# A two-layer diffusion backbone on one core: norm sums by tokens on partitions, two final products on GpSimd, and another place for the weight order FOURS

## The chip, the cores and the metric

The kernel runs on one core of one Trainium2 chip. The metric is device time in microseconds, the median of several executions. A profiled execution gives, besides, a trace of each engine: PE (TensorE; PEld is its weight load), DVE (VectorE), ACT (ScalarE), POOL (GpSimd) and SP, whose queue issues the DMAs.

## The reference

256 latent tokens and 256 context tokens of width 2048 pass an even layer (retention and a Fourier mixing, one output projection) and an odd layer (gated short convolution); the latent stream then has a final norm. All is float32. What matters here:

```python
def _rmsnorm(x, w):
    y = x * rsqrt(mean(x * x, axis=-1) + EPS)          # over the 2048 channels of one token
    return y * w
# per layer:  h = _rmsnorm(x, w) * (1 + scale) + shift
# even layer: x = x + gate * (concat(retention, fourier) @ w_out)       4096 -> 2048
# odd layer:  bg, cg, xt, g = split(h @ w_in)                           2048 -> 4 * 4096
#             x = x + gate * ((bg * conv3(cg * xt) * silu(g)) @ w_out)  4096 -> 2048
# output: _rmsnorm(x, final_norm_w)
```

## The kernel before

Activations lie transposed: channels on the 128 partitions, 256 tokens along the free axis. So a projection takes the weights as the stationary operand and the activation as the moving one. To keep float32's accuracy, each number is cut in a high part and a residue: of a weight, `whi` (ScalarE, L94) and `wlo` (VectorE, L59), each 128x512, in rings of six; of an activation, both parts side by side in a tile of 512 columns, high part first.

`group_t` computes 256 output channels. A weight load (`raw`, 1 MB, by SP, three buffers) has four pieces; a piece is one pair `whi`, `wlo`, and eight matmuls: four H (high part of the weight by all 512 columns) and four L (residue by the 256 columns of the high part). Results stand in PSUM in two halves, which `lr` adds. The order of the eight is a table: LOW is L0 H0 L1 H1 L2 H2 L3 H3, HIGH is H0 L0 H1 L1 ..., FOURS is H0 H1 H2 H3 L0 L1 L2 L3. `SETTLE` and `AFTER` name for a call which order its first piece has and which the others have; without them a call has LOW throughout.

`project` is the output projection of either layer (`w0o`, `w1o`): eight blocks of 256 channels, the first seven by `group_t` (four weight loads, 16 pieces, each), the last by `group_d`, which adds in one PSUM bank. It adds gate times result to the stream `x1` (L831) and gathers the squares for the next norm in `acc`. At the end the sum over channels is a product with a matrix of ones, which leaves the sum of each token in all partitions (128x256, bank `tot`); `rstd_bc` takes the root (ScalarE, L206) and the reciprocal (VectorE, L207). In the first layer the row then enters `modulate` (L213 to L215), which makes the input `h` of the second layer's projection `w1` (16 blocks of four groups `tcg`, `txt`, `tbg`, `tg`, eight pieces each). In the second layer it multiplies the stream into `fo` (L62, L920), and eight DMAs (L922), issued by SP in program order, write the output. `fo` is in ring `t2` of five buffers.

During the first layer and its output projection, background tasks read the matrices `adaT` (VectorE, L388) for the gates. The order of instructions on each engine is set by a scheduler from the program, with its own estimate of times; each engine then runs its list in order.

Of the kernel before, what the change touches and what calls it, by code (L numbers as in the profile page):

```python
# [20 lines left out]
D = 2048  # L21
# [3 lines left out]
P = 128  # L25
# [10 lines left out]
def body(tc, a, out):  # L36
    nc = tc.nc
    es = ExitStack()
    with es:
# [9 lines left out]
        def bank(name):  # L49
            return ap.tile([P, 512], F32, tag="bk", name=name)  # L50
# [77 lines left out]
        HIGH = "H0 L0 H1 L1 H2 L2 H3 L3".split()  # L128
        FOURS = "H0 H1 H2 H3 L0 L1 L2 L3".split()

        SETTLE, AFTER = (HIGH, FOURS), (HIGH, LOW)

        def group_t(wd, i0, nkt, streams, orders=(LOW, LOW)):

            ps = [psum("gT") for _ in streams]
            last = nkt * 8 - 1
            for kt in range(nkt):
                raw = load_raw(wd[i0 + kt])
                bg()
                for pc, (hi, lo) in enumerate(split_w(raw)):  # L140
                    todo = orders[kt + pc > 0]
                    seen = set()
                    for what, j in ((x[0], int(x[1])) for x in todo):
                        k2, m = j // 2, j % 2
                        kc, c0 = kt * 8 + pc * 2 + k2, j * 128
                        n = 512 if what == "H" else 256
                        w = (hi if what == "H" else lo)[:, c0:c0 + 128]
                        for t, st in zip(ps, streams):
                            mm(t[:, m, 0:n], w, st[kc // 2][:, kc % 2, 0:n], kc == 0 and j not in seen,
                               kc == last and j in seen)  # L150
                        seen.add(j)
                    if pc % 2:
                        hook()
            return ps
# [667 lines left out]

        finish_mods(0, 16)
        l1 = es.enter_context(tc.tile_pool(name="l1", bufs=1))
        x1 = [l1.tile([P, 2, 256], F32, name=f"x1_{b}") for b in range(8)]

        def project(wd, xs, gcol, xin, acc, first=None, post=None):


            def res(b, m, v, src):  # L830
                nc.vector.scalar_tensor_tensor(x1[b][:, m, :], v, mods[:, gcol + 2 * b + m:gcol + 2 * b + m + 1],  # L831
                                               src[:, m, :], op0=ALU.mult, op1=ALU.add)

            tot = None
            for b in range(8):
                src = xin(b)
                quiet[0] = b >= 7 - (post is not None)
                if b < 7:
                    t = first if b == 0 and first is not None else group_t(wd, 4 * b, 4, [xs], *({1: (SETTLE,), 2: (AFTER,)}.get(b, ())))[0]
                    s = lr(l1, t)  # L840
                    for m in range(2):
                        res(b, m, s[:, m, :], src)
                    if b == 0:
                        nc.scalar.square(acc[:], x1[b][:])
                    else:
                        sq = l1.tile([P, 2, 256], F32, tag="t2", bufs=5, name="sq")
                        nc.scalar.square(sq[:], x1[b][:])
                        add(acc[:], acc[:], sq[:])
                    for m in range(2 if post is not None else 0):
                        nc.scalar.activation(x1[b][:, m, :], x1[b][:, m, :], AF.Copy,  # L850
                                             scale=cols[:, post + 2 * b + m:post + 2 * b + m + 1])
                else:
                    t = group_d(wd, 4 * b, 4, xs)
                    tot = bank("tot")
                    for m in range(2):
                        mm(tot[:, 0:256], ones[:], acc[:, m, :], m == 0, False)

                    warm = l1.tile([P, 1], F32, tag="warm", name="warm")
                    nc.scalar.activation(warm[:], acc[:, 0, 0:1], AF.Sqrt)
                    sq = l1.tile([P, 2, 256], F32, tag="t2", bufs=5, name="sq")  # L860
                    for m in range(2):
                        res(b, m, t[:, m * 256:m * 256 + 256], src)
                        nc.scalar.square(sq[:, m, :], x1[b][:, m, :])
                        mm(tot[:, 0:256], ones[:], sq[:, m, :], False, m == 1)
            return rstd_bc(l1, tot[:, 0:256], D)

        def reload(b):
            xr = l1.tile([P, 2, 256], F32, tag="t2", bufs=5, name="xr")
# [14 lines left out]
        w1 = a["w1"]  # L883
        y1 = []
        for b in range(16):
            tcg, = group_t(w1, b * 8, 2, [h1], *((SETTLE,) if b in (1, 2) else ()))
            scg = lr(l1, tcg, "scg", 2)
            txt, = group_t(w1, b * 8 + 2, 2, [h1], *((AFTER,) if b in (1, 2) else ()))
            z = lr(l1, txt, "z", 2)
            mul(z[:], z[:], scg[:])  # L890
            cv = l1.tile([P, 2, 256], F32, tag="cv", bufs=2, name="cv")
            for m in range(2):
                w = [cols[:, C_CV + j * 32 + 2 * b + m:C_CV + j * 32 + 2 * b + m + 1] for j in range(3)]
                z4 = z[:, m, :].rearrange("p (r w) -> p r w", w=64)
                c4 = cv[:, m, :].rearrange("p (r w) -> p r w", w=64)
                nc.vector.tensor_scalar(cv[:, m, :], z[:, m, :], w[1], None, op0=ALU.mult)
                nc.vector.scalar_tensor_tensor(c4[:, :, 1:64], z4[:, :, 0:63], w[0], c4[:, :, 1:64],
                                               op0=ALU.mult, op1=ALU.add)
                nc.vector.scalar_tensor_tensor(c4[:, :, 0:63], z4[:, :, 1:64], w[2], c4[:, :, 0:63],
                                               op0=ALU.mult, op1=ALU.add)  # L900
            tbg, = group_t(w1, b * 8 + 4, 2, [h1])
            sbg = lr(l1, tbg)
            mul(cv[:], cv[:], sbg[:])
            tg, = group_t(w1, b * 8 + 6, 2, [h1])
            sg = silu_lr(l1, tg, "t2", 5)
            mul(cv[:], cv[:], sg[:])
            y1.append(act_tile(YA[b] if b < 8 else f"hx{b - 8}", f"y1_{b}"))
            split_act(y1[b], cv[:])
            quiet[0] = False

        finish_mods(48, 64)
        acc1 = l1.tile([P, 2, 256], F32, tag="acc", name="acc1")
        rs2 = project(a["w1o"], y1, 48, lambda b: x1[b], acc1, post=C_FNW)
        for b in range(8):
            o = l1.tile([P, 2, 256], F32, tag="t2", bufs=5, name="fo")
            if b < 7:
                mul(o[:], x1[b][:], rs2[:].unsqueeze(1).to_broadcast([P, 2, 256]))
            else:
                for m in range(2):
# [20 lines left out]
def _layout(i):  # L940
# [37 lines left out]
    wu = w0[:, uo:uo + 2048].reshape(2048, 8, 256)  # L978
    m = np.concatenate([[128], np.arange(255, 128, -1)])
    wu = np.stack([wu[:, :, 0:128], wu[:, :, m]], axis=1)  # L980
    a["w0m"] = wu[:, :, :, 0].reshape(16, P, 2, 8).transpose(1, 0, 2, 3)
    wu = wu.reshape(8, 2, P, 2, 2, 4, P).transpose(4, 0, 2, 1, 3, 5, 6)
    a["w0u"] = wu.reshape(16, P, 2048)
# [49 lines left out]
```

## Time and profile before

| | |
|---|---|
| median of 3 runs | 1823.37 us (1822.88, 1823.37, 1826.58) |
| profiled execution | 1826.86 us; its span, first to last instruction, 1825.1 us |
| busy share of PE, DVE, ACT, POOL | 97%, 68%, 49%, 0% |
| granted TensorE clock | 0.988 |
| first layer's output projection, blocks 1 to 7 | about 763 to 914 us of the span |
| first layer's closing norm and `modulate` | 914 to 937 us |
| `w1` / `w1o` | 920 to about 1630 / to 1812 us |
| closing norm and output | 1812 to 1825 us |

A row of a group reads: line, engine, operation, what it writes <- reads, shapes, count, then busy us, mean ns of one, and idle time of the engine before it with what ended it. A row of a stretch gives its bounds, its length, busy us with the number of instructions, the granted clock, the busy share of the DMA engines and their GB/s.

### The profile page before, as it was taken

Reading aid. Unit: us, or ns where it says so; the run is one execution under the profiler, and the core shown is the slowest. Engines: PE = TensorE matmul, PEld = TensorE weight load, DVE = VectorE, ACT = ScalarE, POOL = GpSimd, SP = SyncE. Lnnn points to the kernel's source line nnn. Section 1 sums busy time; section 2 is a strip of 40 time slices with the busy share of each in tenths; the row PEclk is TensorE's granted clock in tenths of the full one; section 3 lists DMA queues with packets and bytes.
Section 4 is the critical chain, followed back from the end, with each engine's and each line's share of the span. In section 5 each row is a group of like instructions: output and inputs, shape, how many; then the busy total and the mean of one; then the engine's idle time right before and its main releaser. Section 6 shows DMA issues by size and latency. Waiting matters only on the chain.

```text
span 1825.1 us, 25950 instructions
## 1 busy us (share of the span) xinstructions
PE 1777.8 (97%) x10086; PEld 1514.6 (83%) x10086; DVE 1248.0 (68%) x2001; ACT 901.9 (49%) x1493; POOL 0.2 (0%) x4
## 2 busy tenths in 40 slices
PE   5999999999989999999999999999999999999997
PEld 3667888888877888888978888888888888888887
DVE  5348858758469788777677888666666666665554
ACT  4225626345455455444555555555555555555553
POOL 0000000000000000000000000000000000000000
PEclk9999999999989899999999999999999999999999
DMA  9886656655435556577647777555555555555552
GB/s 388 341 315 259 233 212 221 240 207 208 166 117 217 199 188 216 194 295 295 231 155 264 296 277 281 197 191 185 187 196 195 185 185 191 197 189 185 187 193 105
DMA packets 58732, 400.82 MB, mean 220 GB/s; under 512 B 6512, under 2 KB 6896, under 8 KB 11376
## 3 DMA queue, kind: packets, MB, share of 16 engines
q1 hardware_dynamic: 58608, 399.16, 59.8%
q8 instruction: 79, 1.29, 0.3%
q14 instruction: 45, 0.37, 0.1%
HBM read 397.03 MB, written 2.10 MB: 219 GB/s over the span
## 4 chain that ended last, share of the span: by engine, by line
PE 94%; DVE 3%; DMA 1%; ACT 1%; issue 0%; SPq 0%; DVEq 0%; ACTq 0%
PE gT L56 71%; PE gN L56 7%; PE gD L56 3%; PE pu L56 2%; PE gemv L56 2%; PE o L56 2%; PE pk L56 1%; PE pvx L56 1%; PE pvc L56 1%; PE pd L56 1%; DMA raw<-ada 1%; PE S L56 1%; PE pq L56 1%; DVE wlo L59 1%; PE pP L56 1%; PE py L56 0%
## 5 line engine op out<-in xcount | busy, mean ns | idle before, releaser
L94 ACT CAST whi<-raw 128x512 fp32r<-128x512 f32 x1024 | 628.3, 620 | 627.3 <-PE gT L56 469.4
L59 DVE TENSOR_TENSOR wlo<-raw,whi 128x512 fp32r<-128x512 f32 x1024 | 693.2, 688 | 344.4 <-ACT whi L94 334.5
L56 PE MATMUL gT<-h,whi 128*128 128x512 f32 x2048 | 707.6, 394 | 0.7 <-DVE h L215 0.7
L56 PE MATMUL gT<-h,wlo 128*128 128x256 f32 x2048 | 560.8, 278 | 3.4 <-ACT h L214 3.4
L56 PEld LDWEIGHTS gT<-h,whi 128*128 128x128 f32 x2048 | 383.3, 188 | 89.0 <-DVE h L215 1.2
L56 PEld LDWEIGHTS gT<-h,wlo 128*128 128x128 f32 x2048 | 383.4, 188 | 5.6 <-ACT h L214 3.8
L56 PE MATMUL gT<-hx,whi 128*128 128x512 f32 x576 | 209.4, 398 | 0.0
L388 DVE CUSTOM_DVE_ANT_0 raw<-raw,scb 128x2048 f32<-128x2048 f32 x64 | 146.5, 2290 | 54.0 <-DMA raw<-adaT 50.8
L56 PE MATMUL gT<-hx,wlo 128*128 128x256 f32 x576 | 165.2, 287 | 2.8 <-ACT v L507 1.6
L56 PE MATMUL gT<-y,whi 128*128 128x512 f32 x448 | 150.9, 394 | 0.0
L56 PEld LDWEIGHTS gT<-hx,whi 128*128 128x128 f32 x576 | 108.8, 189 | 21.3
L56 PEld LDWEIGHTS gT<-hx,wlo 128*128 128x128 f32 x576 | 109.5, 190 | 10.0 <-DVE wlo L59 2.7
L56 PE MATMUL gT<-y,wlo 128*128 128x256 f32 x448 | 116.9, 278 | 0.0
L56 PEld LDWEIGHTS gT<-y,whi 128*128 128x128 f32 x448 | 82.9, 188 | 18.2
L198 ACT COPY lr_r<-gT 128x512 f32<-128x512 f32 x103 | 60.5, 587 | 65.7 <-PE gT L56 65.4
L56 PEld LDWEIGHTS gT<-y,wlo 128*128 128x128 f32 x448 | 82.1, 188 | 1.4
L56 PE MATMUL gT<-yA,whi 128*128 128x512 f32 x224 | 77.5, 398 | 0.0
L56 PE MATMUL gT<-yB,whi 128*128 128x512 f32 x224 | 76.9, 398 | 0.0
L65 DVE TENSOR_TENSOR t<-gT,lr_r 128x512 f32<-128x512 f32 x68 | 46.9, 689 | 29.9 <-ACT lr_r L198 29.7
L56 PE MATMUL gT<-yA,wlo 128*128 128x256 f32 x224 | 59.9, 281 | 0.6 <-DVE wlo L59 0.6
L56 PE MATMUL gN<-whi,hx 128*128 128x512 f32 x192 | 59.7, 392 | 0.0
L56 PE MATMUL gN<-whi,hc 128*128 128x512 f32 x192 | 59.7, 391 | 0.0
(283 smaller groups left out, 2162.0 us busy)
## 6 DMA issues: line engine op xcount, KB each, us to landing
raw<-w SPq DMA_DIRECT2D x168, 1024.0 KB, 4.8
raw<-adaT SPq DMA_DIRECT2D x64, 1024.0 KB, 4.9
raw<-ada SPq DMA_DIRECT2D x32, 1024.0 KB, 7.1
raw<-w0o SPq DMA_DIRECT2D x32, 1024.0 KB, 4.8
raw<-w1o SPq DMA_DIRECT2D x32, 1024.0 KB, 4.8
raw<-w0g SPq DMA_DIRECT2D x16, 1024.0 KB, 4.8
raw<-w0u SPq DMA_DIRECT2D x16, 1024.0 KB, 4.9
raw<-w0s SPq DMA_DIRECT2D x8, 1024.0 KB, 5.6
```

Source lines behind the costliest of these rows:

```text
L56: nc.tensor.matmul(o, l, r, start=start, stop=stop, skip_group_check=True)
L59: nc.vector.tensor_tensor(o, x, hi.bitcast(F32), op=ALU.subtract)
L65: nc.vector.tensor_tensor(o, x, y, op=ALU.add)
L94: nc.scalar.copy(hi, x)
L198: nc.scalar.copy(r[:], t[:, :, 256:512])
L388: nc.vector.tensor_tensor_reduce(out=raw[:], in0=raw[:], in1=scb[:], scale=1.0, scalar=0.0, op0=ALU.mult, op1=ALU.add, accum_out=gv[:, j:j ...
```

## The change

Three things. First, the closing norm of both layers: the squares are now the stationary operand and one column of ones the moving one, so a token's sum stands on a partition (128x2, one column for each half of the tokens). Root and reciprocal are taken of that, and the row is brought back to all partitions by two products with an identity matrix `eye` (a new input, loaded once), which leave it in PSUM (`tot[:, 256:512]`), where `modulate` and the final products read it. Second, at the end ScalarE copies the row to SBUF (`rsb`), and GpSimd computes the final products of blocks 1 and 4. Third, `SETTLE` and `AFTER` become lists of eight orders, one for each piece, and stand elsewhere: in `project` in blocks 3 and 4 (eight pieces SETTLE, eight AFTER) instead of 1 and 2, in `w1` in groups `tbg`, `tg` of blocks 0 and 1 besides `tcg`, `txt` of blocks 1 and 2.

```diff
-        SETTLE, AFTER = (HIGH, FOURS), (HIGH, LOW)
+        SETTLE, AFTER = [HIGH] + [FOURS] * 7, [HIGH] + [LOW] * 7
...
-                    todo = orders[kt + pc > 0]
+                    todo = orders[(kt * 4 + pc) % len(orders)]
...
+        eye = l1.tile([P, P], F32, name="eye")
+        nc.sync.dma_start(eye[:], a["eye"])
...
-                    t = first if b == 0 and first is not None else group_t(wd, 4 * b, 4, [xs], *({1: (SETTLE,), 2: (AFTER,)}.get(b, ())))[0]
+                    t = first if b == 0 and first is not None else group_t(wd, 4 * b, 4, [xs], SETTLE + AFTER if b in (3, 4) else (LOW,))[0]
...
+                    def sums(x, fst, lst):
+                        for h in range(2):
+                            mm(tot[:, h:h + 1], x[:, h * 128:h * 128 + 128], ones[:, 0:1], fst and h == 0, lst)
+
                     for m in range(2):
-                        mm(tot[:, 0:256], ones[:], acc[:, m, :], m == 0, False)
+                        sums(acc[:, m, :], m == 0, False)
...
-                        mm(tot[:, 0:256], ones[:], sq[:, m, :], False, m == 1)
-            return rstd_bc(l1, tot[:, 0:256], D)
+                        sums(sq[:, m, :], False, m == 1)
+            r = l1.tile([P, 2], F32, tag="rcol", bufs=2, name="rcol")
+            nc.scalar.activation(r[:], tot[:, 0:2], AF.Sqrt, bias=eps[:], scale=1.0 / D)
+            nc.vector.reciprocal(r[:], r[:])
+
+            for h in range(2):
+                mm(tot[:, 256 + h * 128:384 + h * 128], r[:, h:h + 1].to_broadcast([P, P]), eye[:], True, True)
+            return tot[:, 256:512]
...
-            tcg, = group_t(w1, b * 8, 2, [h1], *((SETTLE,) if b in (1, 2) else ()))
+            tcg, = group_t(w1, b * 8, 2, [h1], SETTLE if b in (1, 2) else (LOW,))
...
-            txt, = group_t(w1, b * 8 + 2, 2, [h1], *((AFTER,) if b in (1, 2) else ()))
+            txt, = group_t(w1, b * 8 + 2, 2, [h1], AFTER if b in (1, 2) else (LOW,))
...
-            tbg, = group_t(w1, b * 8 + 4, 2, [h1])
+            tbg, = group_t(w1, b * 8 + 4, 2, [h1], SETTLE if b in (0, 1) else (LOW,))
...
-            tg, = group_t(w1, b * 8 + 6, 2, [h1])
+            tg, = group_t(w1, b * 8 + 6, 2, [h1], AFTER if b in (0, 1) else (LOW,))
...
+        rsb = l1.tile([P, 256], F32, tag="rstd", name="rsb")
+        nc.scalar.copy(rsb[:], rs2[:])
         for b in range(8):
             o = l1.tile([P, 2, 256], F32, tag="t2", bufs=5, name="fo")
-            if b < 7:
+            if b in (1, 4):
+
+                nc.gpsimd.tensor_tensor(o[:], x1[b][:], rsb[:].unsqueeze(1).to_broadcast([P, 2, 256]), op=ALU.mult)
+            elif b < 7:
                 mul(o[:], x1[b][:], rs2[:].unsqueeze(1).to_broadcast([P, 2, 256]))
```

How it moves instructions, at three places. A row names what is written, then what is read; of a matmul the moving operand stands first, then the stationary one, then the shape of the result.

PE in the first layer's output projection, at the start of its block 3 (`gT_7096` before, `gT_7098` after; `yA` is the layer's activation). Before, first two pieces in part:

```order
L56 MATMUL gT_7096<-yA0_1510,wlo_7103 128x256
L56 MATMUL gT_7096<-yA0_1510,whi_7102 128x512
L56 MATMUL gT_7096<-yA0_1510,wlo_7103 128x256
L56 MATMUL gT_7096<-yA0_1510,whi_7102 128x512
L56 MATMUL gT_7096<-yA0_1510,wlo_7103 128x256
L56 MATMUL gT_7096<-yA0_1510,whi_7102 128x512
```

After, the end of the first piece and the next two:

```order
L56 MATMUL gT_7098<-yA0_1510,whi_7104 128x512
L56 MATMUL gT_7098<-yA0_1510,wlo_7105 128x256
L56 MATMUL gT_7098<-yA1_1514,whi_7108 128x512 x4
L56 MATMUL gT_7098<-yA1_1514,wlo_7109 128x256 x4
L56 MATMUL gT_7098<-yA2_2404,whi_7112 128x512 x4
L56 MATMUL gT_7098<-yA2_2404,wlo_7113 128x256 x4
```

The first piece is now HIGH and the next seven FOURS, then one HIGH and seven LOW; block 4 has the same again, and block 1, which had FOURS, has LOW.

PE after the first layer's norm, where it waits for VectorE, with the first two groups of `w1` interleaved (`gT_8322` and `gT_8427` before, `gT_8330` and `gT_8435` after; `h1_4` is a part of the modulated input, two slices of 128 channels). Before:

```order
L56 MATMUL gT_8322<-h1_4_8254,wlo_8376 128x256
L56 MATMUL gT_8322<-h1_4_8254,whi_8375 128x512
L56 MATMUL gT_8322<-h1_5_8255,wlo_8380 128x256
L56 MATMUL gT_8427<-h1_0_8250,wlo_8431 128x256
L56 MATMUL gT_8427<-h1_0_8250,whi_8430 128x512
```

After:

```order
L56 MATMUL gT_8330<-h1_4_8262,wlo_8384 128x256
L56 MATMUL gT_8435<-h1_0_8258,wlo_8439 128x256
L56 MATMUL gT_8435<-h1_0_8258,whi_8438 128x512
L56 MATMUL gT_8435<-h1_0_8258,wlo_8439 128x256
L56 MATMUL gT_8435<-h1_0_8258,whi_8438 128x512
```

The second group's first piece now stands ahead of the H matmuls of the second half of `h1_4`.

VectorE and GpSimd at the end, in the closing norm and output. VectorE before:

```order
L207 RECIPROCAL rstd_17091<-rstd_17091 128x256
L62 TENSOR_TENSOR fo_17094<-x1_0_6640,rstd_17091 128x512
L62 TENSOR_TENSOR fo_17097<-x1_1_6641,rstd_17091 128x512
L62 TENSOR_TENSOR fo_17100<-x1_2_6642,rstd_17091 128x512
L62 TENSOR_TENSOR fo_17103<-x1_3_6643,rstd_17091 128x512
L62 TENSOR_TENSOR fo_17106<-x1_4_6644,rstd_17091 128x512
```

After, VectorE's rows and, last three, all that GpSimd has after its start-up:

```order
L874 RECIPROCAL rcol_17103<-rcol_17103 128x2
L62 TENSOR_TENSOR fo_17110<-x1_0_6642,tot_17087 128x512
L62 TENSOR_TENSOR fo_17116<-x1_2_6644,tot_17087 128x512
L62 TENSOR_TENSOR fo_17119<-x1_3_6645,tot_17087 128x512
L62 TENSOR_TENSOR fo_17125<-x1_5_6647,tot_17087 128x512
L933 ISA
L933 TENSOR_TENSOR fo_17113<-x1_1_6643,rsb_17108 128x512
L933 TENSOR_TENSOR fo_17122<-x1_4_6646,rsb_17108 128x512
```

Products 1 and 4 moved to GpSimd behind a library step (`ISA`); SP's list still issues the eight outputs in the order of blocks. VectorE's product 0 waits for the semaphore count of ScalarE's copy `rsb`, as GpSimd's product 1 does; product 5 waits for the landing of output 0, product 6 for that of output 1, and the last for that of output 2.

More of the change, by code (lines that the diff above doesn't have):

```diff
@@ L129, in body, with group_t @@
         FOURS = "H0 H1 H2 H3 L0 L1 L2 L3".split()
-        SETTLE, AFTER = (HIGH, FOURS), (HIGH, LOW)
-        def group_t(wd, i0, nkt, streams, orders=(LOW, LOW)):
+        SETTLE, AFTER = [HIGH] + [FOURS] * 7, [HIGH] + [LOW] * 7
+        def group_t(wd, i0, nkt, streams, orders=(LOW,)):
             ps = [psum("gT") for _ in streams]
@@ L980, in _layout @@
     wu = np.stack([wu[:, :, 0:128], wu[:, :, m]], axis=1)
+    a["eye"] = np.eye(P, dtype=np.float32)
     a["w0m"] = wu[:, :, :, 0].reshape(16, P, 2, 8).transpose(1, 0, 2, 3)
```

## The prediction

> **What bounds the kernel now.** I read the page's busy shares and the shares of the chain that ended last first, then the chain piece by piece at the places that the change touches, then the count of matmuls in equal stretches.
>
> ```profile
> PE 1777.8 (97%) x10086; PEld 1514.6 (83%) x10086; DVE 1248.0 (68%) x2001; ACT 901.9 (49%) x1493; POOL 0.2 (0%) x4
> PE 94%; DVE 3%; DMA 1%; ACT 1%; issue 0%; SPq 0%; DVEq 0%; ACTq 0%
> ```
>
> TensorE is the bound nearly everywhere, so an edit counts in two ways only: where the chain leaves PE (the two closing norms), and where it alters the pace at which PE issues. The last norm, in the chain in order of time (start, length, what):
>
> ```profile
> 1812.20 0.49 DVE x L831
> ...
> 1812.72 0.42 ACT sq L863
> ...
> 1813.19 1.15 PE tot L56 x4
> ...
> 1814.36 0.48 ACT rstd L206
> ...
> 1814.86 1.76 DVE rstd L207
> ...
> 1816.65 2.82 DVE fo L62 x5
> ...
> 1820.90 0.48 DVE fo L920
> ```
>
> The reader sees one series without overlap; the reciprocal of 128x256 is its dearest single step. The first layer has the same series at 914.8, and after it VectorE holds PE back until 928.8, from where PE has the chain again. The last three rows are PE's: its wait in the middle of the series (in square brackets), its pace after that (busy, matmuls, clock), and its last wait for VectorE:
>
> ```profile
> 916.44 0.48 ACT rstd L206
> ...
> 916.94 1.76 DVE rstd L207
> ...
> 918.73 1.28 DVE modt L213 x3
> ...
> 928.34 0.41 DVE h L215
> ...
> 928.79 16.29 PE gT L56 x91
> 919.81 0.44 PE L56 MATMUL gT<-h,wlo 128*128 128x256 f32 x1 [3.41 <-ACT h L214]
> 920.00:923.40 3.40, 3.19 (x10) 0.50 0.00 0
> 928.79 0.50 PE L56 MATMUL gT<-h,whi 128*128 128x512 f32 x1 [0.47 <-DVE h L215]
> ```
>
> Pace of PE, from stretches counted on PE alone (us, busy, matmuls, clock, DMA):
>
> ```profile
> 785.00:885.00 100.00, 100.00 (x567) 1.00 0.79 294
> 1025.00:1125.00 100.00, 100.00 (x579) 1.00 0.76 283
> 1500.00:1600.00 100.00, 100.00 (x579) 1.00 0.54 190
> 1657.00:1677.00 20.00, 20.00 (x116) 1.00 0.53 190
> ```
>
> All four are fully busy at full clock, yet the first issues fewer matmuls. About two matmuls in each count only overlap an edge, so one takes 100/565 = 177.0 ns in the first layer's output projection and 100/577 = 173.3 ns in the second layer's input projection (second and third row); in order FOURS (last row) 20/114 = 175.4 ns. In LOW order there are thus two paces, 3.7 ns a matmul or 29 ns a piece (8 matmuls) apart. The slow one is not a shortage: DMA load is alike in the first two rows. It follows what stood before: the quick rows come after one HIGH piece, seven FOURS, one HIGH, LOW.
>
> **The change, part by part, against the profiled execution (1826.86 us, span 1825.1).**
>
> Sums by tokens. The four 128x256 products per norm become eight one-column products, each of two passes. The nearest row is the modulation's, also fp32 with 128x128 weights:
>
> ```profile
> L56 PE MATMUL gemv<-cols,gs 128*128 128x2 f32 x64 | 7.7, 242 | 0.8 <-DVE gs L287 0.8
> L56 PE MATMUL tot<-sq,ones x8: 379/379/483, 915.3 to 1813.9; 128*128 128x256 f32 x8
> L56 PEld LDWEIGHTS tot<-sq,ones x8: 186/188/190, 915.3 to 1813.7; 128*128 128x128 f32 x8
> L859 ACT ACTIVATE warm<-acc 128x1 f32<-128x1 f32 x2 | 0.4, 202 | 0.0
> L65 DVE TENSOR_TENSOR md<-gemv,cols 128x4 f32<-128x4 f32 x16 | 1.8, 157 | 8.0 <-PE gemv L56 7.8
> L207 DVE RECIPROCAL rstd<-rstd 128x256 f32<-128x256 f32 x1 | 1.8, 1753 | 1.8 <-ACT rstd L206 1.8
> L863 ACT ACTIVATE sq<-x 128x256 f32<-128x256 f32 x2 | 0.8, 416 | 8.7 <-DVE x L831 8.7
> ```
>
> Its 64 passes are eight in each of eight calls: 7.7/8 = 0.96 us a call, 0.12 a pass. The eight on the closing squares begin as before at 1813.19 and, with some 0.2 for a first load that nothing hides, end at 1814.35: no gain over 1814.34. Those on acc stand before the squares and are hidden by the residual and the square (1812.2 to 1813.1). Root over 128x2: 0.20 like the warm-up row, for 0.48. Reciprocal over 128x2: 0.17, near VectorE's row of 4 columns (157 ns), for 1.76. Its low end is 0.06; its high end, 1.75 again, holds if the price is per call, but VectorE's rows grow with their columns (157 ns for 4, 684 for 512 below). The new step: two products with the identity, four passes of 128 columns, the first load 0.19, three more starts at 0.12, and 0.31 from start to end of the last (between 242 and 379): 0.86. With three hand-overs of 0.03, the row stands in PSUM at 1814.35 + 0.20 + 0.17 + 0.86 + 0.09 = 1815.67, against 1816.62 (1814.86 + 1.76) before: -0.95 us. Bounds: four passes at the 0.38 of a 256-column one without overlap (1.5) leave -0.3; 0.5 for all four gives -1.3; a reciprocal at 1.75 would turn -0.95 into +0.6.
>
> First layer: the same -0.95, then the modulation reads the row from PSUM. VectorE's chain from 918.73 to 928.79 moves as a whole. The order puts one more weight residue ahead of the second half of h_4, but on PE one piece of the second group now fills that place, and its operand stands behind 9.8 us of VectorE work (20 steps of the modulation at 0.40, 3 residues at 0.60, the starts of this chain), where the old one stood behind 10.0. PE was there 0.47 us early before, so -0.95 stays. The identity's DMA (64 KB, issued ahead of xr on SP, which passes one w0o load) costs nothing while the weight slots are full; if a weight comes late for it, some 0.2.
>
> Second layer: the first product on VectorE does not start when the row stands. It waits for ScalarE's copy of the row, by the same semaphore value as GpSimd's product. A copy of 128x256 is near the 0.42 of the square, plus 0.06 for two hand-overs: VectorE starts at 1816.15, not 1816.65: -0.5. Were the copy free, -0.95; at the 0.59 of a 512-column copy, -0.3.
>
> GpSimd. What do two products fewer on VectorE bring (they start 0.60 apart)? The output queue answers:
>
> ```profile
> DMA  0000000000029999999999999999999700000000
> L922 SPq DMA_DIRECT2D out<-fo x8: 332/333/348, 1817.4 to 1821.8; - x8
> DMA to landing us min/median/max: 2.0/2.4/2.6
> ```
>
> The first row (40 slices of 1815 to 1826) is full from 1818.3 to 1823.5: 2.1 MB leave at the DMA engines' pace, 0.68 us per 256 KB, nearly VectorE's 0.60. Also fo has five buffers, so products 5, 6, 7 wait until outputs 0, 1, 2 have landed. Let S be the start of the products (1816.65 now) and g the time of one on GpSimd. The last output now lands at 1821.8 + 2.4 = S+7.55. SP takes the outputs in order, so output 1 and all behind it wait for GpSimd: issued at S+g, landed 2.05 later, six more at 0.69, S+g+6.2. Output 4, its second: S+2g + 2.05 + 3 x 0.69 = S+2g+4.1. The largest counts. Up to g = 1.35 GpSimd costs nothing and gains nothing. No row prices it: 0.69 (VectorE's own row, 682/684/694) is the low end, 3.5 (the reciprocal's pace for 512 columns) the high, giving 0 to +3.6. It is a plain product, nearest the low end; I take 1.3 and so 0. The Trainium skill (GPSIMD Engine Reference, Performance versus the Vector engine) puts such an operation at 1.96 times VectorE's. By it g would be an estimated 1.35 us, which changes the sum by nothing; no run here shows it yet.
>
> Fours. In w0o pieces of blocks 3 to 6 (64) were all slow. Now 14 are FOURS (175.4: 14 x 8 x 1.6 ns = -0.18), 4 HIGH (0 taken), and 46 LOW, quick if the sequence does there what it does in w1: 46 x 29 ns = -1.35 (else 0). Block 1 loses its FOURS, which other products cut apart: 0, ends 0.2 either way; block 2 stays LOW. Together -1.5. In w1, blocks 0 and 1 change 32 pieces between FOURS, slow and quick, -0.1; in w1o two FOURS stretches replace one, 0.
>
> In block 1 of w0o, PE stands for a residue that is late behind a VectorE step waiting for its DMA:
>
> ```profile
> DVE raw L388 <- DMA raw<-adaT: 2.3, 1, 2.3
> PEld gT L56 <- DVE wlo L59: 0.9, 1, 0.9
> ```
>
> LOW begins with the residue, FOURS did not, and the order of this step changes; -0.8 to +0.9, taken 0.
>
> Sum: -0.95 - 0.5 - 1.5 - 0.1 = -3.05, so 1823.8 for such an execution. The profiled one stands 3.5 above the median of 1823.37; one timed run, 1826.58, stands with it. If these are two levels of pace, the median already has some quick pieces and can't gain the 1.5 twice. The 80 pieces of w0o's blocks 2 to 6 alone hold 80 x 29 ns = 2.3 of the 3.5, so I let half of the 1.5 count: 1823.37 - 1.55 - 0.75 = 1821.1.
>
> **The rivals.**
> 1. All of it counts. The levels come from elsewhere, the order change gives its whole 1.5, and the stall of 0.8 goes: 1823.37 - 3.05 - 0.8 = 1819.5. For it: the first row's 100 us, in blocks 2 to 6, are slow throughout. Against: the unexplained level, and that the stall is a DMA's.
> 2. GpSimd is slow. At g = 3.5 the end moves by S+11.1 for S+7.55, +3.6: 1824.7. It decides from 1.35 on. For it: no row of POOL but 0.2 us of start-up. A heavier form is a start of h before GpSimd's first product: it holds output 1, SP's queue and product 6, so 1821.1 + h, slower by over 0.2% from h = 5.9; the order shows the library step at the head of POOL's program, 1800 us ahead, which speaks against it. The Trainium skill (GPSIMD Engine Reference, Instruction dispatch) speaks of about 6 us at the first call of a freshly loaded kernel, by which the sum would be an estimated 1827; no row here shows such a start.
> 3. The quick pace is lost (slower than before). Re-entering HIGH after 7 LOW pieces, where before there were 23, may leave w1 in the slow pace: blocks 2 to 15 (448 pieces) and w1o up to its own HIGH (48), 496 x 29 ns = +14.4: 1835.5. Over the 2.3 gained and 3.65 (0.2%) it decides from 205 slow pieces on. Against: by the rows at 1025 and 1500 the pace, once quick, held.
> 4. The change doesn't do what it says: four passes without overlap, a slow copy, w0o as now: -0.3 in the first norm, +0.3 in the second, so 1823.4.
>
> A rule on the clock, the row first: PE idles 3.41 us in the first norm, and the stretch behind it shows 10 matmuls in 3.4 us at clock 0.50. The Trainium skill (TensorE: Matmul & The Clock Gate, What's actually happening) says an idle window of about 3.4 us halves the clock; with the idle time cut to some 2.5 us, the drop could go by it. By the last wait PE still stood 0.47 us for VectorE afterwards, so with or without the drop the sum is the same.
>
> **How the numbers follow.** A change under 0.2% (3.65 us) can't be told from none in this kernel. Forecast 0.47, own range 1819.8 to 1822.4 (all or none of the 1.5, half of the row's bounds). Rival 1 0.30, rival 2 0.08 for slow and 0.03 for the heavy start, rival 3 0.07, rival 4 0.05. Faster by over 0.2% means under 1819.7: rival 1, 0.30. Slower, over 1827.0: rival 3 and two thirds of the heavy start, 0.09. The rest, 0.61, is within. The range reaches from 1818.3 (rival 1, the row at both its -1.3 ends, the level of the lowest run, 0.5 under the median) to 1825.4 (rival 2's slow form without w0o's part); outside it stay the heavy start, rival 3 and a few in a hundred at the low end.
>
> **What would show it.** Right: 2.2 us from the end of the first layer's last square to its first modulation step, now 3.1; VectorE's first output product behind ScalarE's copy, 0.5 after the row; DMA full through the output as now; 577 matmuls net in 100 us of w0o's late blocks and of w1. Wrong: a product of POOL over 1.35, an idle stretch in the output's transfers, slow counts in w1, a new wait of PE in block 1 of w0o.

## Result and profile after

The changed kernel takes 1835.07 us (median of 1834.48, 1835.03, 1835.11, 1838.86) against 1823.12 us for the kernel before on the same chip (1822.84, 1822.88, 1823.37, 1826.58). The ratio is 1.0066, 95% interval 1.0047 to 1.0084. The forecast was 1821.1, in a range of 1818.3 to 1825.4; the kernel became slower instead of faster, and the time lies near that of rival 3 (1835.5).

The page of the profiled execution after (1835.11 us, span 1833.3, clock 0.991), busy shares and the shares of the chain that ended last:

```profile
PE 1788.6 (98%) x10110; PEld 1520.1 (83%) x10110; DVE 1243.7 (68%) x1999; ACT 901.8 (49%) x1494; POOL 2.7 (0%) x6
PE 95%; DVE 3%; DMA 1%; ACT 1%; issue 0%; SPq 0%; DVEq 0%; ACTq 0%
```

PE is busy 10.8 us longer than before, for 24 matmuls more. Its counts in the stretches that the prediction read (us, busy, matmuls, clock, DMA):

```profile
785.00:885.00 100.00, 100.00 (x569) 1.00 0.77 286
1025.00:1125.00 100.00, 100.00 (x568) 1.00 0.75 280
1500.00:1600.00 100.00, 100.00 (x568) 1.00 0.52 184
```

All three stand near the 567 of the slow pace; before, the last two had 579. So `w0o` did not become quick, and `w1` lost the quick pace that it had. (From 1025 to 1745 us, which takes in part of `w1o`, PE has 4079 matmuls against 4154 before.)

The closing norm in the chain in order of time (start, length, what), then the output's DMA row (40 slices of 1823 to 1834) and GpSimd's group:

```profile
1822.21 1.07 PE tot L56 x8
...
1823.30 0.27 ACT rcol L873
...
1823.59 0.18 DVE rcol L874
...
1823.81 0.72 PE tot L56 x4
...
1824.56 0.38 ACT rsb L928
...
1824.96 0.70 DVE fo L62
...
1825.68 2.05 DMA out<-fo
```

```profile
DMA  0000000000001999999999999999999980000000
L933 POOL TENSOR_TENSOR fo<-x,rsb x2: 1264/1265/1266, 1825.0 to 1826.2; 128x512 f32<-128x512 f32 x2
```

The series is shorter, the stream of the output as full as before, and GpSimd's two products run beside VectorE's. The first norm, from the same view, and the clock behind it:

```profile
910.22 1.07 PE tot L56 x8
...
911.83 0.72 PE tot L56 x4
...
912.57 1.26 DVE modt L213 x3
...
914.29 15.81 PE gT L56 x74
```

```profile
913.20:920.00 6.80, 6.29 (x18) 0.50 0.00 0
```

The whole difference, by when the same instruction stands in the two traces (us):

| up to | before | after | added in the piece |
|---|---|---|---|
| first matmul of `w0o` on `yA` | 712.16 | 708.08 | -4.08 |
| end of the first norm's squares | 915.61 | 910.56 | -0.97 |
| 38th matmul of `w1` on `h` | 928.79 | 923.28 | -0.45 |
| end of the last squares | 1813.53 | 1822.55 | +14.52 |
| first product of `fo` | 1816.65 | 1824.96 | -0.71 |
| end of the span | 1825.08 | 1833.33 | -0.06 |

The first row is, as far as the traces tell, not the change: in the ten traces of kernels with the new norm this instruction stands anywhere from 707.68 to 714.55, in the four with the old one from 710.27 to 712.95. Stretches of before and then of after show another clock there:

```profile
541.20:551.30 10.10, 8.91 (x22) 0.50 0.34 112
633.40:636.70 3.30, 3.30 (x11) 0.50 0.00 0
```

```profile
541.20:551.30 10.10, 7.68 (x36) 1.00 0.44 144
633.40:636.70 3.30, 3.30 (x23) 1.00 0.14 27
```

At half clock PE did 22 matmuls for 36, and 11 for 23. Up to 715 us the trace of before has 34.1 us at half clock, that of after 17.1. Such stretches come in other lengths in each execution; they fit that the profiled execution of before stands 3.7 us over its median and that of after at it, and that of after's four runs the one with the lowest clock, 0.987, is the longest (1838.86; the others have 0.990 to 0.992). So 8.25 in the spans and 11.95 in the medians are one result, and its cause is the 14.5 us of `w1` and `w1o`. Of the second row, 0.86 goes with a wait of PE in the profiled execution of before, in `w0o`'s block 1: `norm_pool` and `before_six` (below), which have before's order in `w0o` but not the wait, take 202.59 us for this piece, before 203.45 and after 202.48.

### The profile page after: what moved, and what is told of

The parts are those of the page before. It is cut to its first block, busy times and chain, and to the rows that moved or that the text cites. A ratio compares the mean times of both kernels' runs of the same rounds, so it can differ in the third digit from the quotient of the medians.

```text
span 1833.3 us, 26023 instructions
## 1 busy us (share of the span) xinstructions
PE 1788.6 (98%) x10110; PEld 1520.1 (83%) x10110; DVE 1243.7 (68%) x1999; ACT 901.8 (49%) x1494; POOL 2.7 (0%) x6
## 4 chain that ended last, share of the span: by engine, by line
PE 95%; DVE 3%; DMA 1%; ACT 1%; issue 0%; SPq 0%; DVEq 0%; ACTq 0%
PE gT L56 71%; PE gN L56 7%; PE gD L56 3%; PE pu L56 2%; PE gemv L56 2%; PE o L56 2%; PE pvx L56 1%; PE pk L56 1%; PE pvc L56 1%; PE pd L56 1%; PE S L56 1%; PE pq L56 1%; PE pP L56 1%; PE py L56 1%; PE pz L56 1%; DVE wlo L59 1%
## 5 line engine op out<-in xcount | busy, mean ns | idle before, releaser
L59 DVE TENSOR_TENSOR wlo<-raw,whi 128x512 fp32r<-128x512 f32 x1024 | 694.3, 688 | 359.0 <-ACT whi L94 353.3
L56 PE MATMUL gT<-h,whi 128*128 128x512 f32 x2048 | 716.3, 399 | 0.1
L56 PE MATMUL gT<-yB,wlo 128*128 128x256 f32 x224 | 62.4, 281 | 0.0
```

The source lines that it names most:

```text
L56: nc.tensor.matmul(o, l, r, start=start, stop=stop, skip_group_check=True)
L59: nc.vector.tensor_tensor(o, x, hi.bitcast(F32), op=ALU.subtract)
```

## Experiments

A settle below is a run of pieces HIGH, FOURS (several), HIGH, then LOW. A pair is one L matmul and the H matmul behind it; a LOW piece has four. The kernel before was measured again beside each group of runs, so its median differs from group to group.

The expectations weigh three theories against each other. By the phase theory, the pace behind a settle depends on the pieces at which its FOURS start and end, and so on their number. By the norm theory, the new norm shifts the start of `w1` and this alone takes the quick pace. By the count theory, more settles are better, but not when they stand close together.

**Which part costs it?** Three kernels divide the change, and a fourth tries the phase theory in its first form, by which the number of FOURS decides.

`norm_pool`: the change with all tables of before (new norm row, copy, GpSimd alone).

> The changed kernel with all tables of the kernel before: the new norm sums and GpSimd's two products alone. Phase theory: w1 quick as in the kernel before; the norm gains what the profile after showed, 0.45 us at layer 1's end and 0.7 at the end of the kernel: 1821.5 to 1823. Norm theory: w1 slow, 1835 to 1838.

`orders_only`: the kernel before with the new tables alone.

> The kernel before with the new tables alone (w0o's and w1's), without the new norm sums and without GpSimd. Phase theory: no H is pulled forward in the order, all settles are HIGH and seven FOURS from a slow pace, so w1 and w1o stay slow: 13 to 15 us over the kernel before, 1836 to 1838. Norm theory: the quick pace of the kernel before is kept, 1822 to 1824.

`w1_as_before`: the change with `w1`'s two new settles taken out.

```diff
-            tbg, = group_t(w1, b * 8 + 4, 2, [h1], SETTLE if b in (0, 1) else (LOW,))
+            tbg, = group_t(w1, b * 8 + 4, 2, [h1])
-            tg, = group_t(w1, b * 8 + 6, 2, [h1], AFTER if b in (0, 1) else (LOW,))
+            tg, = group_t(w1, b * 8 + 6, 2, [h1])
```

> The changed kernel with the two w1 tables tbg and tg back to LOW, so that only tcg and txt of blocks 1 and 2 settle, as in the kernel before; the norm row, GpSimd's two products and w0o's tables stay changed. The order puts one H matmul of the HIGH piece (gT_8765 H) one piece forward again, as before. Phase theory (what the FOURS leave behind depends on the piece at which they start and end): the LOW pieces of w1 from block 1 on and of w1o go at the quick pace, 346.7 ns a pair instead of 353.3; 496 pieces by some 26 to 29 ns less than after, 13 to 14.5 us: 1820 to 1822. Norm theory (the norm's other end shifted the start of w1, and this took the quick pace): the tables do nothing, the slow pace stays, 1834 to 1836. Count theory (more settles are better, only those that stand too close to each other fail): block 1 alone at 7 LOW pieces from block 2's, some of w1 quick, 1822 to 1830.

`six_last`: one FOURS fewer in `w1`'s last settle, with a LOW piece in its place.

```diff
+        SIX = [HIGH] + [FOURS] * 6 + [LOW]
-            tcg, = group_t(w1, b * 8, 2, [h1], SETTLE if b in (1, 2) else (LOW,))
+            tcg, = group_t(w1, b * 8, 2, [h1], SIX if b == 2 else SETTLE if b == 1 else (LOW,))
```

> The changed kernel with six FOURS pieces instead of seven (and a LOW piece in the eighth place) in the last settle of w1, tcg of block 2; everything else as after. Phase theory (FOURS pieces alternate between two patterns, the LOW pace behind them is set by which of the two came last, and a settle that begins at the slow pace begins with the first): an odd number leaves slow as slow, an even number turns slow into quick. Then w1 from block 2 on and w1o go at 346.7 ns a pair: some 30 of 32 parts of the 14.5 us come back, 1820.5 to 1822.5, and HIGH of block 2's txt keeps it quick. Count theory (the settles come too close, or seven LOW pieces between FOURS and the next HIGH do it) and norm theory: 1834 to 1836 as after, since one piece of FOURS less changes neither.

Measured against before (1823.73): `norm_pool` 1838.11, ratio 1.0076 (1.0061 to 1.0091); `orders_only` 1840.24, 1.0088 (1.0070 to 1.0106); `w1_as_before` 1837.62, 1.0077 (1.0061 to 1.0094); `six_last` 1839.02, 1.0082 (1.0067 to 1.0097). All four are slow, so three of my four expectations on the phase theory missed: either half of the change alone loses the quick pace, and `w1`'s old tables don't bring it back. Among these kernels the quick pace of before is thus the exception, and the theory needs the entry, the pair behind which the settle begins, as well as the number. The traces show it. `norm_pool` and before have the same order of matmuls at this settle (an H pulled one piece forward). PE in order of time, before:

```profile
965.53 0.40 PE L56 MATMUL gT<-h,whi 128*128 128x512 f32 x1
965.76 0.28 PE L56 MATMUL gT<-h,wlo 128*128 128x256 f32 x1
965.88 0.63 PE L56 MATMUL gT<-h,whi 128*128 128x512 f32 x2
966.35 0.28 PE L56 MATMUL gT<-h,wlo 128*128 128x256 f32 x1
966.46 0.39 PE L56 MATMUL gT<-h,whi 128*128 128x512 f32 x1
```

and `norm_pool`:

```profile
962.75 0.28 PE L56 MATMUL gT<-h,wlo 128*128 128x256 f32 x1
962.86 0.40 PE L56 MATMUL gT<-h,whi 128*128 128x512 f32 x1
963.09 0.28 PE L56 MATMUL gT<-h,wlo 128*128 128x256 f32 x1
963.21 0.64 PE L56 MATMUL gT<-h,whi 128*128 128x512 f32 x2
963.69 0.28 PE L56 MATMUL gT<-h,wlo 128*128 128x256 f32 x1
963.80 0.39 PE L56 MATMUL gT<-h,whi 128*128 128x512 f32 x1
```

The two H in one row (x2) are where HIGH begins. The intervals from start to start, taken with more digits, differ there. In ns, letter and interval to the next matmul:

```
slow LOW pace, three pairs and again:  L117 H241 L120 H236 L113 H233     1060 = 353.3 a pair
quick LOW pace, three pairs:           L117 H231 L113 H232 L118 H230     1041, mean 346.7 a pair
before, into HIGH at 965.8:            .. L113 H232 | H236 L116 H224 L118 H233 ..
norm_pool, into HIGH at 963.1:         .. L117 H241 | H237 L117 H230 L117 H230 ..
FOURS, pattern A, behind its first H:  H233 H236 H224 L118 L120 L120 L120
FOURS, pattern B, behind its first H:  H236 H228 H232 L118 L119 L118 L116
```

FOURS pieces alternate A, B, A, B in every trace (the first of `six_high`'s last settle, below, has intervals of its own in A's place, H226 H227 H227 L113 L118 L120 L121). The quick LOW cycle repeats after two pairs, to within 1 ns, so a piece of four always ends at the same place of it. The slow cycle has three pairs, so the pair behind which HIGH begins depends on how many pieces went before and, it seems, on where the stalls at the start of `w1` left the cycle. Read over all traces: entered behind L113 H233 or L117 H241, the FOURS begin with A; behind L120 H236, or from the quick pace, with B. After a last B, HIGH and LOW go quick; after a last A, slow. (With the H pulled forward, HIGH lasts eight pairs, and L113 leads to B, as in before.) So an odd number hands on the pace it met, but for one slow entry in three, L120 H236, from which it leads to the quick pace. An even number turns the pace over; from that third entry it should leave slow as slow, which no run shows. In `six_last` the six did end with B (L117 L119 L118 L116), but LOW right behind put two L together, and the pace was slow, in this one trace.

**The number of FOURS, with HIGH behind them.** `six_high` puts HIGH behind the six; `before_six` does the same in the kernel before, where the settle begins quick; `six_b0` has only two settles, and `low_all` none. The edit of `six_high`, then in short those of `six_b0` and `low_all`:

```diff
+        SIX = [HIGH] + [FOURS] * 6 + [HIGH]
-            tcg, = group_t(w1, b * 8, 2, [h1], SETTLE if b in (1, 2) else (LOW,))
+            tcg, = group_t(w1, b * 8, 2, [h1], SIX if b == 2 else SETTLE if b == 1 else (LOW,))
-            txt, = group_t(w1, b * 8 + 2, 2, [h1], AFTER if b in (1, 2) else (LOW,))
+            txt, = group_t(w1, b * 8 + 2, 2, [h1], AFTER if b in (1,) else (LOW,))
```

> The changed kernel, but the last settle of w1 (block 2) is HIGH, six FOURS, HIGH instead of HIGH, seven FOURS, HIGH; all pieces behind it are LOW as in after, and all settles ahead of it stay. In the run with six FOURS and a LOW piece right behind them, the FOURS had ended in the pattern (L117 L119 L118 L116) that the quick pace follows in the kernel before, but LOW put two L products together there. Phase theory: with HIGH behind the sixth FOURS the pace is 346.7 ns a pair from 1023 us on, through w1 and w1o: some 720 us by 1.9% come back, 13.5 us of after's 1835: 1820.5 to 1823. Rivals (the quick pace needs the norm's old end, or fifteen or more pieces between settles, or one settle only): 1834 to 1839, as all runs so far but the kernel before.

> The kernel before, but its second settle of w1 (block 2), which begins at the quick pace, is HIGH, six FOURS, HIGH instead of HIGH, seven FOURS, HIGH. Phase theory: a settle that begins quick begins with the other pattern, so an even number ends with L120 L120 L120 and leaves the slow pace: 1023 us to the end at 353.3 ns a pair, 13 to 14.5 us lost, unless the settle of w1o turns it back: 1835 to 1838. Rivals: one FOURS piece fewer changes nothing that can be measured, 1821 to 1826.

```diff
# six_b0: in project, in w1's tbg; all other calls LOW
+ group_t(wd, 4 * b, 4, [xs], SIX + [LOW] * 8 if b == 3 and post is None else (LOW,))[0]
+ tbg, = group_t(w1, b * 8 + 4, 2, [h1], SIX if b == 0 else (LOW,))
# low_all
+ SETTLE, AFTER = [LOW] * 8, [LOW] * 8
```

> The changed kernel with two settles only: HIGH, six FOURS, HIGH in w0o's block 3 and in w1's block 0 (tbg); everything else LOW. Phase theory: both begin at the slow pace (all settles of after did), so both turn it quick: w0o's blocks 4 to 6 gain 1.9% of some 90 us, 1.7 us; w1 is quick from 960 us on, 15 us against after, and stays so through w1o if nothing there stalls PE for long: 1817.5 to 1820. If w1 begins quick because w0o ended quick, its settle turns it slow: 1833 to 1836. Rivals as for the other two: 1834 to 1839.

> The changed kernel with LOW in every piece: no settle at all. Phase theory: the pace is whatever the stalls at the start of w1 leave, which was the slow one in all six traces so far: 1834 to 1838 by the slow pace without the FOURS' own price. A rival to which settles always help (each seven FOURS that are left out cost): over 1838.

Measured against before (1825.50): `six_high` 1824.27, ratio 0.9988 (0.9978 to 0.9999); `before_six` 1836.43, 1.0062 (1.0046 to 1.0078); `six_b0` 1820.33, 0.9975 (0.9966 to 0.9985); `low_all` 1838.12, 1.0073 (1.0057 to 1.0088). Three of these times lie 0.1 to 1.3 us above the ranges that I had given, in runs in which before itself stood 2.4 us higher than beside the changed kernel; by the signs and sizes the theory held. The stretch 1025 to 1125 of `six_high`, then of `before_six`:

```profile
1025.00:1125.00 100.00, 100.00 (x579) 1.00 0.76 285
```

```profile
1025.00:1125.00 100.00, 100.00 (x568) 1.00 0.77 284
```

One FOURS fewer turns slow into quick in the one kernel and quick into slow in the other: the phase theory held with both signs. Theories on the norm, the number of settles or their distance, by which nothing or the same sign would follow, fall. Places in `six_high` agree: PE from 1025 to 1745 us has 4154 matmuls, as in before, against 4079 after; 75 x 173.3 ns = 13.0 us. `w1o`'s settle of fifteen FOURS in `before_six`, of which the expectation had left this open, turned quick again at 1687; it was entered behind L120 H235. In `low_all` the slow pace goes through to the end; against it the times show no worth of the seven-FOURS settles of after (ratios 1.0073 and 1.0066, intervals that overlap). Its 1838.12 is 0.12 over the bound that I had named for a theory by which settles always help; in the traces, from the 38th matmul of `w1` on `h` to the last squares, it takes 0.6 us more than after (899.89 and 899.26).

In `six_b0` both settles turn quick. `w0o` from 765 to 885, in after and then in `six_b0`:

```profile
765.00:885.00 120.00, 120.00 (x682) 1.00 0.77 285
```

```profile
765.00:885.00 120.00, 120.00 (x690) 1.00 0.78 291
```

Eight matmuls more, 1.4 us: what the Fours term had wanted of `w0o`. With an interval of 0.9966 to 0.9985 this version is faster than the kernel before, by a quarter of a per cent.

**The entry, with the number kept.** `plus1` and `plus2` begin the changed kernel's last settle of `w1` one or two LOW pieces later, still with seven FOURS (n is 1 or 2).

```diff
+        PLUS = [LOW] * n + [HIGH] + [FOURS] * 7 + [HIGH] + [LOW] * (7 - n)
+            tcg, = group_t(w1, b * 8, 2, [h1], PLUS[:8] if b == 2 else SETTLE if b == 1 else (LOW,))
+            txt, = group_t(w1, b * 8 + 2, 2, [h1], PLUS[8:] if b == 2 else AFTER if b == 1 else (LOW,))
```

> The changed kernel with the last settle of w1 (block 2) begun one LOW piece later; it keeps HIGH, seven FOURS, HIGH. The slow LOW pace repeats after three pairs (L117 H241, L120 H236, L113 H233) and a piece has four pairs, so one piece more moves the settle's entry one pair on: from behind L113 H233, where after entered it, to behind L117 H241. Phase theory with three entries, read from the traces so far: behind L113 H233 and behind L117 H241 the FOURS begin with H L L L ending in L120 L120 L120 (pattern A), behind L120 H236 with L117 L119 L118 L117 (pattern B); patterns alternate, and the pace behind the last is quick after B, slow after A. So seven FOURS from behind L117 H241 end in A: slow, 1833 to 1839. Its rival (a settle later in block 2 is better, or worse, by its place): no difference between this kernel and the next.

> The changed kernel with the last settle of w1 (block 2) begun two LOW pieces later; it keeps HIGH, seven FOURS, HIGH. Two pieces more move the entry two pairs on, to behind L120 H236. By the three entries the FOURS begin with pattern B there, seven of them end with B, and the pace from 1028 us on is quick: 13 to 13.5 us less than after, 1821 to 1825. Rivals (an odd number of FOURS keeps slow as slow wherever it stands; the place of a settle doesn't matter): 1833 to 1839.

Measured against before (1823.93): `plus1` 1834.25, ratio 1.0056 (1.0039 to 1.0073); `plus2` 1823.35, 0.9994 (0.9985 to 1.0004). Both as expected. The counts, `plus1` and then `plus2`:

```profile
1025.00:1125.00 100.00, 100.00 (x568) 1.00 0.76 277
```

```profile
1025.00:1125.00 100.00, 100.00 (x579) 1.00 0.77 283
```

One LOW piece's difference in place, with no instruction added or removed, is 11 us in the medians, of which that of `plus1` is of two runs. In the traces, over the same piece as above, it is 13.0: 898.14 us in `plus1` and 885.10 in `plus2`, against 899.26 in after and 884.74 in before. (`w1o`'s settle in `plus1` was entered behind L120 H236 and turned quick, which is why it stands 1.1 below after.) By the intervals `plus1` enters behind L117 H241 and ends with A, `plus2` behind L120 H236 and ends with B. Over the thirteen traces that have FOURS, 72 stretches of four or more of them stand behind 700 us; in 71 the pace behind is quick after B and slow after A, and the one exception is that of `six_last`.

**The norm and GpSimd at the same pace.** `six_vec` is `six_b0` without the copy and without GpSimd; `six_old_norm` is the kernel before with `six_b0`'s two settles alone.

```diff
-        rsb = l1.tile([P, 256], F32, tag="rstd", name="rsb")
-        nc.scalar.copy(rsb[:], rs2[:])
-            if b in (1, 4):
-                nc.gpsimd.tensor_tensor(o[:], x1[b][:], rsb[:].unsqueeze(1).to_broadcast([P, 2, 256]), op=ALU.mult)
-            elif b < 7:
+            if b < 7:
```

> The kernel with two settles of six FOURS (w0o's block 3, w1's block 0), without the copy of the last norm's row and without GpSimd: all final products on VectorE, reading the row in PSUM. In the trace after, GpSimd's two products took 1265 ns each, hidden beside VectorE's, and the output stream stood full from the first piece on. Theory (the stream sets the end, the copy's 0.3 to 0.4 us stand ahead of it): within 0.5 us of the same kernel with GpSimd, 0.9973 to 0.9980 of before. If GpSimd's share did gain, 0.7 to 2 us more: 0.9979 to 0.9986. The paces aren't touched.

> The kernel before with those two settles of six FOURS alone: old norm sums, no GpSimd. It tells what the norm row and GpSimd are worth at the same pace: the trace after had 0.45 us less at layer 1's end and 0.7 at the kernel's, so 1.2 us over the kernel with both, 0.9979 to 0.9985 of before, if both settles are entered in one of the two phases from which six FOURS lead to the quick pace. If the old norm brings w1's settle to the third phase (behind L120 H236), w1 stays slow from 960 us on: 1.006 to 1.008.

Measured against before (1823.93): `six_vec` 1819.66, ratio 0.9981 (0.9971 to 0.9991); `six_old_norm` 1821.63, 0.9984 (0.9975 to 0.9992). The time of `six_vec` lies in the range that I had given for a gain by GpSimd, but its interval covers the other range too, and the three versions can't be told apart by their times. By their traces they can, from the end of the last squares to the end of the span: 11.56 us in `six_old_norm` (11.55 in before), 10.79 in `six_b0`, 10.58 in `six_vec`. The last 0.2 needs care. The closing chain of `six_vec`:

```profile
1807.97 0.92 PE tot L56 x4
...
1808.92 2.82 DVE fo L62 x5
```

From the start of the products with the identity to VectorE's first product it is 0.95 us, and 1.15 with the copy (1823.81 to 1824.96 in after). But the products with the identity took 0.92 here and 0.72 in after: in `six_vec` the clock fell to 0.50 at 1808.35, within them. So the copy costs more than 0.20: from the end of these products to VectorE's start it is 0.03 in `six_vec` and 0.43 in after, 0.40 more. From the first product to the end it is 8.37 us in `six_vec` and in `six_b0`: GpSimd's two products themselves gain nothing and cost nothing, and the copy, which only they need, is a loss.

## Why the prediction was wrong

- **The Fours term failed**, in the step "46 LOW, quick if the sequence does there what it does in w1" and in "-0.1" for `w1`. I had read the quick pace as following "one HIGH piece, seven FOURS, one HIGH, LOW". It follows the pattern of the last FOURS, which depends on entry and number. The three rows that I had quoted could not tell these apart, since both stretches in `w1` hung on one settle. The intervals were in the trace of before: the last four FOURS in a row of `w0o`'s block 1, where other products cut them apart, and the seven of `w1`'s settles both begin with B; the four end with A and slow, the seven with B and quick. I had not read the intervals.
- Instead of -1.5, `w0o`'s order gave -0.1 (202.48 us against the 202.59 of the two kernels with the old order and no wait), and instead of -0.1, `w1` with `w1o` gave +14.5.
- **Rival 3 named the mechanism's place and price**: 496 pieces by 29 ns, +14.4, 1835.5. Its reason, seven LOW pieces between settles instead of 23, isn't the cause as such. `norm_pool` and `w1_as_before` have 23 and are slow; `plus2` has nine and is quick. Behind a settle that ends slow, the first LOW piece has intervals of its own and the next six are 24 pairs, a multiple of three, so the changed kernel's settles kept meeting the cycle behind L113 H233 and stayed slow. That the price came out to 0.1 us is luck: a piece is 4 x 6.6 = 26.4 ns slower, not 29, and the slow pace went on behind `w1o`'s own HIGH, through 46 LOW pieces more; some 540 x 26.4 ns are 14.3 us. The chance of 0.07 was too small: of the three slow entries, two lead to the slow pace behind seven FOURS.
- **"Two levels of pace" was wrong.** What parts the executions is, as far as the traces show, the length of the stretches at half clock. By the times, each program kept to one pace of PE in all its runs, though only one run of each was traced. Halving the 1.5 had no ground.
- **The norm row** was right in kind: squares to first modulation step 3.12 to 2.01, -1.11 for -0.95. What reaches PE was 0.45 in this execution. Here the clock statement failed: I said that with or without the drop PE would still stand for VectorE. After the drop PE is slow from 913.2 to 920.0 and has the chain from 914.29 on. Over the ten traces with the new norm the piece from the squares to the 38th matmul took 11.84 to 12.76 us, against 13.18 or 13.19 in the four with the old: a gain of 0.42 to 1.34. The clock parts them: it was at 0.50 for 6.8 us in eight of the ten, which took 12.34 to 12.76, and for 3.4 us in the two others (`six_last`, `six_vec`), which both took 11.84.
- **The closing norm** gained 0.71 for the predicted 0.5: the row stood 1.10 earlier instead of 0.95, mostly because the products with the identity took 0.72 for the 0.86 taken, and the copy took back 0.40 instead of 0.45. Five other traces with the copy have the 0.71 within 0.01. The three others (`norm_pool`, `six_last`, `low_all`) gained 0.19 to 0.41: there the clock fell to 0.50 before or within the products with the identity, which took 1.02 to 1.24 us.
- **GpSimd's products** were priced right: 1.265 us against 1.3 taken, under the break-even of 1.35. The Trainium skill (GPSIMD Engine Reference, Performance versus the Vector engine) gives 1.96 times VectorE; this trace has 1265 against 687 ns, 1.84 times. The 6 us at a first call of which the Trainium skill speaks (GPSIMD Engine Reference, Instruction dispatch) don't show: the first product starts at 1825.0, beside VectorE's at 1824.96, and one took 1.264 us, the other 1.266.
- **Block 1 of `w0o`** (taken 0, -0.8 to +0.9): the wait for the late residue (0.9 us of PEld in before, of which PE itself stood 0.6) is gone in after, but PE waits 1.02 us there in `six_b0`, which has the same order in this block; and `norm_pool` and `before_six`, with the order of before, don't have it. It goes with the execution, not with the change.

## What to carry to other kernels

A pace that depends on what stood before is a state. Before moving or copying a sequence that seems to set it, find out from the intervals at its entry what it does from each state; a copy that worked once may have worked from one entry in three. Look for an order that leads to the good state from the state which the kernel is known to be in (here an even number of FOURS from the slow pace, in the two entries of three from which it was run), and look at the intervals again after every edit ahead of it. Such an effect can swamp the edit: 1.2 us of real gain in two norms stood against 14.5 us of a state that the same edit happened to lose.

## What the hardware showed that I had not expected

- PE's alternation of 256- and 512-column matmuls, each with its own weights, runs at two stable paces, 346.7 and 353.3 ns a pair, with the same instructions, at full clock, for over 700 us, and by the times the same program lands in the same one in each run (lowest run of any program with a slow `w1` 1833.2, highest of before 1829.8). What in the chip holds the three-pair cycle stays open; no run takes that apart.
- The order within a piece passes the state on, to a few nanoseconds of each interval: in all 72 stretches the FOURS end in two patterns by turns.
- The clock fell to 0.50 in after's first norm though none of PE's waits there was long; all that stand between the squares and the first matmuls of `w1`:

```profile
910.22 1.05 PE L56 MATMUL tot<-ones,sq 128*128 128x1 f32 x8 [0.24 <-ACT sq L870]
911.83 0.71 PE L56 MATMUL tot<-eye,rcol 128*128 128x128 f32 x4 [0.55 <-DVE rcol L874]
913.65 0.58 PE L56 MATMUL gT<-h,wlo 128*128 128x256 f32 x1 [1.12 <-ACT h L214]
```

The Trainium skill (TensorE: Matmul & The Clock Gate, What's actually happening) has the clock halved after an idle window of about 3.4 us. The waits here add up to 1.9 us, with products of one and of 128 columns between them, and the clock fell all the same, for 6.8 us instead of the 3.4 of before; it fell in all ten traces with the new norm. So waits with such small products between them didn't keep it up here; whether it is the products or the waits, no run tells.
